# Where the second block's memory is projected, and in which order the first block's mixers get their projections

## Chip, cores and metric

One Trainium2 chip, one core of it. The metric is device time in microseconds (us), the median of repeated executions. The profile is one execution taken by the hardware profiler. PE is TensorE, DVE is VectorE, ACT is ScalarE, POOL is GpSimd, SP is the queue that issues most DMAs.

## What is computed

Two transformer blocks on 512 tokens of width 1024, all in float32 (batch 1, depth 1). The first block, cut to what matters:

```python
h = rms_norm(x, norm_mix_gain)
sb_q, sb_k, sb_v, hg_q, hg_f, hg_i, hg_g, mem_q = jnp.split(h @ w_in, split_points, axis=-1)
sb_o = rms_norm(stick_breaking_attention(sb_q, sb_k, sb_v), sb_out_gain)        # 8 heads of 64
hg_o = rms_norm(hgrn2_recurrence(hg_q, hg_f, hg_i, lb), hg_out_gain) * silu(hg_g)  # 4 heads, keys 128, values 64
mem_k, mem_v = jnp.split(rms_norm(mem, mem_norm_gain) @ w_mem_kv, 2, axis=-1)   # 256 memory rows
mem_o = memory_attention(mem_q, mem_k, mem_v, mem_q_gain, mem_k_gain)           # 4 heads
x = x + jnp.concatenate([sb_o, hg_o, mem_o], axis=-1) @ w_out
x = x + peer_ffn(rms_norm(x, norm_ffn_gain), ...)      # 16384 experts, 8 heads, 16 of them each
```

The second block, on the x that the first one leaves:

```python
q, k, v, qm, gate = split(rmsnorm(x, norm_g_2) @ w_in_2)
mix = dilated_window_mixer(q, k, v)                                # 3 groups of 4 heads
kv = rmsnorm(mem_2, mem_norm_g_2) @ w_mem_kv_2                     # does not depend on x
y = concat([mix, full_softmax_attention(qm, kv)]) * silu(gate)
out = rmsnorm(x + y @ w_out_2, final_norm_g_2)
```

## The kernel before

**Projections.** A float32 matrix product is made of three products of rounded halves (hi·hi, hi·lo, lo·hi). `weight` and `split` (L97 to L114) load one slice of a weight matrix, 1024 x 256, in two DMAs of 512 KB (`w_raw`, 3 buffers); ACT makes the upper half (L108), POOL or DVE the lower half (L109). In the first block there are two sets of `w_hi` and `w_lo`, so two slices are ready at a time; there POOL makes the lower halves. `mm_feat` (L116) gives a slice with features on the partitions: 2 groups of 24 matmuls with 512 columns. `mm_tok` (L126) gives it with tokens on the partitions: 4 groups of 24 matmuls with 256 columns. Both go over the input in 8 chunks of 128 features (kc). `to_feat` (L136) makes their input: per chunk it transposes the blocks of 128 rows on PE, then ACT writes the upper half (L151) and DVE the lower (L152).

**First block** (`first`, L421). The rows of x are loaded and normalized (`norm_rows`: square sum on ACT, a small operation on DVE, a power on POOL (L95), a product on DVE (L161)). All four blocks are transposed together, chunk by chunk. Then in the order of the program (L556 to L576): the recurrence's values `tok(10)`; `stick_in(0)`, which is query, key and value slice of the first half of the stick-breaking mixer (`feat(0)`, `feat(2)`, `tok(4)`); the mixer `stick(0)`; `hgrn_in(0)` (two slices for two heads of the recurrence); head 0; `stick_in(1)`; head 1; the rows of the memory; `stick(1)`; `hgrn_in(1)`; heads 2 and 3; the recurrence's gate `tok(11)`; the memory's queries `tok(12)` and `mem_q`; the memory's keys and values `mem_kv`; the second block's memory `mem_2`, whose result goes to DRAM (`kvd`); the memory attention `mem_out`; `hgrn_out`. `stick` works through 10 pairs of blocks (query block qb, key block kb): scores on PE (L285), a chain over DVE and ACT (L290 to L301), a cumulative sum on PE (L303 to L306), again DVE and ACT, and after each query block the product with the values (L314). A head of the recurrence has 7 levels, each of DVE, ACT and PE (L343 to L356). Then `to_feat(mixed)`, the output projection (four slices of `w_out`), and x is stored to DRAM (`x1`).

**What sets the order.** The program is written in one sequence; a scheduler, when the program is built, gives each engine its own fixed queue. An earlier line goes first where both are ready by its reckoning; work of later lines fills the rest. On the chip each queue runs in order. Tiles of one name share a fixed number of buffers (`bufs`), and a new tile waits until the old one has been read for the last time. For the change these matter: `sb_qz`, `sb_kT` and `sb_v` (2 buffers each: the mixer's inputs, and in turn the memory's rows), `hg_qf` (1 buffer: the recurrence's inputs, and before also the memory's upper half), the two weight sets.

**The loop of the experts** (`peer`, L653): 128 iterations over blocks of 128 experts, one product `first_product` (L625 to L627) until iteration 95 and 18 matmuls (L672) each. Beside it POOL gathers rows of `peer_u` and `peer_v` for the first token block (`gather`), and DVE multiplies and adds them (L882, L887). At iteration 100 `keep` (L685) takes the buffer `xT_hi` for x and loads three blocks of `x1` and the second block's projected memory.

**Second block** (`second`, L893): x is normalized (L912), transposed (L914), projected slice by slice from `tok(6)` on; `featT(0)` is next. Its lower halves are made on DVE.

Of the kernel before, what the change touches and what calls it, by code (L numbers as in the profile page):

```python
# [9 lines left out]
F32 = mybir.dt.float32  # L10
# [11 lines left out]
NB = S // P  # L22
# [63 lines left out]
class Body:  # L86
# [39 lines left out]
    def mm_tok(self, ps, w, xt, t0):  # L126

        nc = self.nc
        (wh, wl), (xh, xl) = w, xt
        for kc in range(KC):  # L130
            a, b = xh[:, kc, t0:t0 + P], xl[:, kc, t0:t0 + P]
            nc.tensor.matmul(ps, a, wh[:, kc, :], start=kc == 0, stop=False)  # L132
            nc.tensor.matmul(ps, a, wl[:, kc, :], start=False, stop=False)  # L133
            nc.tensor.matmul(ps, b, wh[:, kc, :], start=False, stop=kc == KC - 1)  # L134

    def to_feat(self, rows, nblk, hi, lo, gain, psums):  # L136

        nc = self.nc
        n = nblk * P
        for kc in range(KC):  # L140
            pool, tag = psums[kc % len(psums)]
            ps = pool.tile([P, 512], F32, name=tag)
            for b in range(nblk):
                nc.tensor.transpose(ps[:, b * P:(b + 1) * P], rows[b][:, kc * P:(kc + 1) * P], self.ident)
            src, h, l = ps[:, :n], hi[:, kc, :], lo[:, kc, :]
            if gain is None:
                nc.scalar.activation(h, src, AF.Copy)
                nc.vector.tensor_tensor(l, src, h.bitcast(F32), op=OP.subtract)
            else:
                g = self.vec[:, gain + kc:gain + kc + 1]  # L150
                nc.scalar.activation(h, src, AF.Copy, scale=g)  # L151
                nc.vector.scalar_tensor_tensor(l, src, g, h.bitcast(F32), op0=OP.mult, op1=OP.subtract)  # L152
# [54 lines left out]
    def mem_kv_2(self, xt, kT, v, wpool, psm):  # L207

        nc = self.nc
        wk = self.weight("w_mem_kv_2", 0, wpool, 2, nc.gpsimd)  # L210
        for c in range(2):
            ps = psm.tile([P, 512], F32, name="mm")
            self.mm_feat(ps[:, :256], wk, xt, c * P)
            nc.scalar.activation(kT[:, c, :], ps[:, :256], AF.Copy)
        wv = self.weight("w_mem_kv_2", 1, wpool, 2, nc.gpsimd)
        for b in range(2):
            ps = psm.tile([P, 512], F32, name="mm")
            self.mm_tok(ps[:, :256], wv, xt, b * P)
            nc.vector.tensor_copy(v[:, b, :], ps[:, :256])

# [53 lines left out]
    def stick(self, g, qz, kT, v, mixed, pool, psa, pso):  # L274
# [146 lines left out]
    def first(self, cp, gp, xr):  # L421
        nc, tc, A = self.nc, self.tc, self.A
        with ExitStack() as es:
# [40 lines left out]
            vi = pool.tile([P, NB, 256], F32, name="hg_i")  # L464
            rows = []
            for n in range(2):
                x2 = tp.tile([P, 2, D], F32, name="sb_qz", bufs=2)
                for b in range(2):
                    nc.sync.dma_start(x2[:, b], A["x"][(2 * n + b) * P:(2 * n + b + 1) * P, :])
                    r = xr.tile([P, D], F32, name="xrow", bufs=4)  # L470
                    self.norm_rows(x2[:, b], r, tp)
                    rows.append(r)
            self.to_feat(rows, NB, hi, lo, V_GMIX, [(psa, "att"), (phg, "hs")])
            mixed = [xr.tile([P, D], F32, name="xrow", bufs=4) for _ in range(NB)]

# [16 lines left out]
            def mem_2(xt):  # L492
                kT = tp.tile([P, 2, 256], F32, name="sb_kT", bufs=2)
                v = tp.tile([P, 2, 256], F32, name="sb_v", bufs=2)
                self.mem_kv_2(xt, kT, v, wpool, psm)
                nc.sync.dma_start(self.kvd[:, :2], kT)
                nc.sync.dma_start(self.kvd[:, 2:], v)
# [10 lines left out]
            def stick_in(eng, g):  # L508
                qz = tp.tile([P, 2, 2, S], F32, name="sb_qz", bufs=2)
                kT = tp.tile([P, 2, S], F32, name="sb_kT", bufs=2)  # L510
                v = tp.tile([P, NB, 256], F32, name="sb_v", bufs=2)
                self.zero_pads(qz, eng)
                feat(g, qz, 0.125)
                feat(2 + g, kT)
                tok(4 + g, slabs(v))
                return qz, kT, v
# [39 lines left out]
            tok(10, slabs(vi))  # L556
            sb = stick_in(nc.vector, 0)
# [3 lines left out]
            hin = hgrn_in(0)  # L561
            hgrn(0, *hin)
# [17 lines left out]
            self.to_feat(mixed, NB, hi, lo, V_GOUT, [(phg, "hs")])  # L580
# [3 lines left out]
            for i in range(4):  # L584
                w = self.weight("w_out", i, wpool)
                for b in range(NB):
                    ps = psm.tile([P, 512], F32, name="mm")
                    self.mm_tok(ps[:, :256], w, (hi, lo), b * P)
                    xs = self.x[b][:, i * 256:(i + 1) * 256]
                    nc.vector.tensor_tensor(xs, xs, ps[:, :256], op=OP.add)  # L590
# [4 lines left out]
    def peer(self, gp, er):  # L595

        nc, tc, A = self.nc, self.tc, self.A
        with ExitStack() as es:
# [46 lines left out]
            with ExitStack() as ec:  # L645
# [7 lines left out]
                for i in range(NE):  # L653
# [21 lines left out]
                    if i == NE - PRE + 4:  # L675
                        self.keep(gp)
# [8 lines left out]
    def keep(self, gp):  # L685
# [4 lines left out]
        for b in range(1, NB):  # L690
# [3 lines left out]
        nc.sync.dma_start(kv, self.kvd)  # L694
# [198 lines left out]
    def second(self):  # L893
        nc, tc, A = self.nc, self.tc, self.A
        with ExitStack() as es:
# [18 lines left out]
            self.to_feat(rows, NB, hi, lo, V_GN2, [(psa, "att")])  # L914
# [199 lines left out]
    def build(self):  # L1114
        nc, tc, A = self.nc, self.tc, self.A
        with ExitStack() as es:
            cp = es.enter_context(tc.tile_pool(name="const", bufs=1, reuse_waits="tile"))
            nc.scalar.preload_act_table_set("natural_log_exp_and_others")
# [13 lines left out]
            self.kvd = dp.tile([P, 4, 256], F32, name="kvd")  # L1132
# [5 lines left out]
            self.second()  # L1138

# [63 lines left out]
```

## Time and profile before

| | us |
|---|---|
| median of 3 runs | 2050.05 (2048.04 to 2053.41) |
| the profiled execution, own time | 2051.2 |
| its span, first to last instruction | 2049.1 |

The profiled execution lies 2.1 us above its span and 1.15 us above the median. In this profile a matmul's end is modelled and neighbours overlap, so what a run of matmuls takes is read from starts, or from a stretch that holds nothing else. "Busy" is the union of an engine's instructions in a stretch. PEclk is the granted TensorE clock as a share of the upper of its two levels (2.4 GHz; the lower is 1.2 GHz). A row of the timeline has the start, the duration, engine, line, operation, output and inputs with shapes, the count, and in brackets the idle time of the engine before it and what ended it.

### The profile page before, as it was taken

How to read it: one execution, taken by the hardware profiler on the slowest of the kernel's cores; microseconds unless marked ns; L12 is line 12 of the kernel's file. 1: busy time of each engine (PE TensorE's matmuls, PEld its weight loads, DVE VectorE, ACT ScalarE, POOL GpSimd, SP SyncE). 2: the span in 40 equal slices, each digit the busy share in tenths (PEclk: the TensorE clock that was granted, in tenths of full speed). 3: DMA queues.
4: the chain of work that ended last, by engine and by line, in shares of the span. 5: the costliest groups of instructions: out<-in, count | busy, mean ns of one | idle time of the engine just before them, and what ended most of it. 6: DMA issues, size and time to landing. Idle time of an engine off the chain costs nothing.

```text
span 2049.1 us, 29902 instructions
## 1 busy us (share of the span) xinstructions
PE 1922.6 (94%) x11285; PEld 1751.1 (85%) x11285; DVE 1413.5 (69%) x2670; ACT 871.8 (43%) x1365; POOL 674.5 (33%) x523
## 2 busy tenths in 40 slices
PE   7999988989688999999999999999999999899997
PEld 6778777989688899899999999999999787789897
DVE  3486875369998976686777777777877676433463
ACT  4564645254346666333333333333433333343442
POOL 4324233076452230043434344334433342113100
PEclk9999999999888999999999999999999999999998
DMA  4211113354324445998889988999898886223211
GB/s 163 71 63 42 42 42 122 122 169 135 103 93 156 184 178 193 311 350 301 295 310 313 316 289 307 316 314 315 308 324 277 279 285 228 93 73 103 74 63 52
DMA packets 150239, 398.19 MB, mean 194 GB/s; under 512 B 12368, under 2 KB 61520, under 8 KB 146896
## 3 DMA queue, kind: packets, MB, share of 16 engines
q1 hardware_dynamic: 110608, 257.83, 37.7%
q0 software_dynamic: 38912, 136.37, 18.5%
q8 instruction: 88, 1.44, 0.3%
q10 hardware_dynamic: 576, 2.10, 0.3%
q14 instruction: 55, 0.45, 0.1%
HBM read 364.23 MB, written 29.88 MB: 192 GB/s over the span
## 4 chain that ended last, share of the span: by engine, by line
PE 61%; DVE 11%; DMA 4%; issue 2%; ACT 1%; POOL 1%; DVEq 0%; POOLq 0%; ACTq 0%
PE o L672 22%; PE hp L626 7%; PE hp L627 7%; PE hp L625 7%; DMA g_row<-peer_v,idx 3%; PE mm L132 2%; PE mm L122 2%; PE mm L123 2%; PE mm L124 2%; PE mm L133 2%; PE mm L134 2%; DVE gated L847 1%; PE g L853 1%; PE g L854 1%; PE mm L854 1%
## 5 line engine op out<-in xcount | busy, mean ns | idle before, releaser
L108 ACT ACTIVATE w_hi<-w_raw 128x1024 fp32r<-128x1024 f32 x366 | 385.7, 1059 | 604.1 <-DMA w_raw<-peer_v 194.4
L109 DVE TENSOR_TENSOR w_lo<-w_raw,w_hi 128x1024 fp32r<-128x1024 f32 x268 | 326.1, 1220 | 92.2 <-ACT w_hi L108 91.5
L625 PE MATMUL hp<-xT_hi,w_hi 128*128 128x384 f32 x1024 | 350.4, 342 | 20.0 <-ACT act L629 20.0
L626 PE MATMUL hp<-xT_lo,w_hi 128*128 128x384 f32 x1024 | 349.5, 341 | 0.0
L627 PE MATMUL hp<-xT_hi,w_lo 128*128 128x384 f32 x1024 | 348.4, 340 | 0.0
L109 POOL TENSOR_TENSOR w_lo<-w_raw,w_hi 128x1024 fp32r<-128x1024 f32 x98 | 245.3, 2511 | 251.5 <-ACT w_hi L108 248.2
L878 POOL DMA_INDIRECT g_row<-peer_u,idx x128 | 169.5, 1324 | 354.5 <-PE o L672 121.5
L878 POOL DMA_INDIRECT g_row<-peer_v,idx x128 | 168.5, 1316 | 264.7 <-PE o L672 116.1
L672 PE MATMUL o<-w_hi,wl 128*128 128x512 f32 x768 | 239.9, 394 | 6.2 <-DVE wl L667 6.2
L672 PE MATMUL o<-w_hi,wh 128*128 128x512 f32 x768 | 240.3, 394 | 2.6 <-ACT wh L666 2.6
L672 PE MATMUL o<-w_lo,wh 128*128 128x512 f32 x768 | 238.8, 392 | 0.0
L882 DVE SCALAR_TENSOR_TENSOR g_row<-g_row,kv 128x1024 f32<-128x1024 f32 x128 | 156.2, 1223 | 94.4 <-DMA g_row<-peer_u,idx 93.8
L625 PEld LDWEIGHTS hp<-xT_hi,w_hi 128*128 128x128 f32 x1024 | 195.9, 191 | 24.2 <-ACT act L629 20.6
L626 PEld LDWEIGHTS hp<-xT_lo,w_hi 128*128 128x128 f32 x1024 | 195.9, 191 | 3.6
L627 PEld LDWEIGHTS hp<-xT_hi,w_lo 128*128 128x128 f32 x1024 | 195.7, 191 | 0.0
L887 DVE SCALAR_TENSOR_TENSOR x<-g_row,dots,x 128x1024 f32<-128x1024 f32 x103 | 132.2, 1283 | 71.6 <-DMA g_row<-peer_v,idx 71.3
L672 PEld LDWEIGHTS o<-w_hi,wl 128*128 128x128 f32 x768 | 144.9, 189 | 38.9 <-DVE wl L667 7.8
L672 PEld LDWEIGHTS o<-w_lo,wh 128*128 128x128 f32 x768 | 145.2, 189 | 32.3
L672 PEld LDWEIGHTS o<-w_hi,wh 128*128 128x128 f32 x768 | 144.0, 189 | 27.2 <-ACT wh L666 2.9
L666 ACT ACTIVATE wh<-act 128x384 fp32r<-128x384 f32 x128 | 67.0, 524 | 221.1 <-PE o L672 220.0
L122 PE MATMUL mm<-xT_hi,w_hi 128*128 128x256 f32 (+1 forms) x384 | 128.8, 336 | 0.4 <-ACT xT_hi L151 0.4
L123 PE MATMUL mm<-xT_lo,w_hi 128*128 128x256 f32 (+1 forms) x384 | 126.2, 329 | 0.0
(340 smaller groups left out, 3881.9 us busy)
## 6 DMA issues: line engine op xcount, KB each, us to landing
w_raw<-peer_uT SPq DMA_DIRECT2D x128, 512.0 KB
w_raw<-peer_v SPq DMA_DIRECT2D x128, 512.0 KB
w_raw<-w_in SPq DMA_DIRECT2D x54, 512.0 KB
gd<-stage SPq DMA_DIRECT2D x24, 1024.0 KB
gt<-gd SPq DMA_DIRECT2D x16, 1536.0 KB
w_raw<-w_query SPq DMA_DIRECT2D x32, 512.0 KB
w_raw<-w_out SPq DMA_DIRECT2D x16, 512.0 KB
w_raw<-w_mem_kv SPq DMA_DIRECT2D x8, 512.0 KB
```

Of the source, the lines that this page charges most:

```text
L108: nc.scalar.activation(hi[:, sl], raw, AF.Copy)
L109: eng.tensor_tensor(lo[:, sl], raw, hi[:, sl].bitcast(F32), op=OP.subtract)
L122: nc.tensor.matmul(ps, a, xh[:, kc, :], start=kc == 0, stop=False)
L123: nc.tensor.matmul(ps, a, xl[:, kc, :], start=False, stop=False)
L625: nc.tensor.matmul(ps, uh[:, kc, :], hi[:, kc, P:], start=kc == 0, stop=False)
L626: nc.tensor.matmul(ps, uh[:, kc, :], lo[:, kc, P:], start=False, stop=False)
L627: nc.tensor.matmul(ps, ul[:, kc, :], hi[:, kc, P:], start=False, stop=kc == KC - 1)
L666: nc.scalar.activation(wh, w, AF.Copy)
L672: last = nc.tensor.matmul(out[b][n], s_[:, sl], m_[:, n * 512:(n + 1) * 512], start=i == 0 and m_ is vh and s_ is wh, stop=i == NE - 1 and ...
L878: dma = nc.gpsimd.indirect_dma_start(out=u, out_offset=None, in_=A["peer_v" if k >= P else "peer_u"], in_offset=bass.IndirectOffsetOnAxis( ...
L882: nc.vector.scalar_tensor_tensor(u, u, 1.0, self.h2, op0=OP.mult, op1=OP.mult, accum_out=dots[:, c:c + 1])
L887: nc.vector.scalar_tensor_tensor(y, u, dots[:, c:c + 1], x, op0=OP.mult, op1=OP.add)
```

## The change

The second block's memory is no longer projected in the first block. In the loop (`keep`) its rows are loaded, normalized and transposed; at the head of `second` its weights are loaded before x is normalized and the products are made after that, before x is transposed. `kvd` is gone. In the first block, `stick_in` makes only queries and keys; the values are projected inside `stick`, after the scores of the first query block. `tok(10)` follows `hgrn_in(0)`. x is transposed in two pairs of blocks. The first memory (`mem_kv`, `tok(12)`, `mem_q`) comes between heads 2 and 3; its upper half lies in buffers of `sb_kT` and `sb_v` (`Halves`) instead of `hg_qf`. `tok(11)` follows `mem_out`. The output projection takes the chunks in the order 0, 1, 2, 3, 6, 7, 4, 5.

```diff
-    def to_feat(self, rows, nblk, hi, lo, gain, psums):
+    def to_feat(self, rows, nblk, hi, lo, gain, psums, group=None, order=range(KC)):
...
+        for b0 in range(0, nblk, group or nblk):
+            here = range(b0, b0 + (group or nblk))
+            t = slice(b0 * P, (b0 + len(here)) * P)
+            for kc in order:
...
+                h, l = hi[:, kc, t], lo[:, kc, t]
...
     def mem_kv_2(self, xt, kT, v, wpool, psm):
-        wk = self.weight("w_mem_kv_2", 0, wpool, 2, nc.gpsimd)
+        wk, wv = (self.weight("w_mem_kv_2", i, wpool, 2, nc.gpsimd) for i in range(2))
+        yield
         for c in range(2):
...
-        wv = self.weight("w_mem_kv_2", 1, wpool, 2, nc.gpsimd)
         for b in range(2):
...
+        yield
...
-    def stick(self, g, qz, kT, v, mixed, pool, psa, pso):
+    def stick(self, g, qz, kT, values, mixed, pool, psa, pso):
...
                 at[kb] = z
+            if qb == 0:
+                v = values()
             for h in range(4):
...
             def mem_in(rows, gain):
-                hi = pool.tile([P, KC, 256], F32R, name="hg_qf", bufs=1)
+                hi = Halves(*(tp.tile([P, KC // 2, 256], F32R, name=n, bufs=2) for n in ("sb_kT", "sb_v")))
                 lo = tp.tile([P, KC, 256], F32R, name="sb_qz", bufs=2)
...
-            self.to_feat(rows, NB, hi, lo, V_GMIX, [(psa, "att"), (phg, "hs")])
+            self.to_feat(rows, NB, hi, lo, V_GMIX, [(psa, "att"), (phg, "hs")], 2)
...
-            tok(10, slabs(vi))
-            sb = stick_in(nc.vector, 0)
+            sb = stick_in(nc.gpsimd, 0)
...
             hin = hgrn_in(0)
+            tok(10, slabs(vi))
             hgrn(0, *hin)
...
             hgrn(2, *hin)
-            hgrn(3, *hin)
-            tok(11, slabs(hg))
+            self.mem_kv(mem_in(normal, V_GMEM), kTm, vm, tp, wpool, psm, pst)
             tok(12, mq)
             mqz = mem_q()
-            self.mem_kv(mem_in(normal, V_GMEM), kTm, vm, tp, wpool, psm, pst)
-            mem_2(mem_in(mem_rows("mem_2"), V_GMEM2))
+            hgrn(3, *hin)
             mem_out(mqz)
+            tok(11, slabs(hg))
             hgrn_out()
...
-            self.to_feat(mixed, NB, hi, lo, V_GOUT, [(phg, "hs")])
+            order = [0, 1, 2, 3, 6, 7, 4, 5]
+            self.to_feat(mixed, NB, hi, lo, V_GOUT, [(phg, "hs")], order=order)
...
-    def keep(self, gp):
+    def keep(self, gp, psh):
...
-        for b in range(1, NB):
+        m = gp.tile([P, 2, KC, 256], F32R, name="xT_lo")
+        rows = []
+        for b, (src, dst) in enumerate(((1, 3), (2, 1))):
+            nc.sync.dma_start(self.x[src], A["mem_2"][b * P:(b + 1) * P, :])
+            self.norm_rows(self.x[src], self.x[dst], self.small)
+            rows.append(self.x[dst])
+        self.mem2 = m[:, 0], m[:, 1]
+        self.to_feat(rows, 2, *self.mem2, V_GMEM2, [(psh, "hp")])
+        for b in (2, 1, 3):
             nc.sync.dma_start(self.x[b], self.x1[b])
         kv = gp.tile([P, 4, 256], F32, name="kv")
-        nc.sync.dma_start(kv, self.kvd)
...
     def second(self):
...
-            b1 = pool.tile([P, 2, 512], F32, name="b1")
-            nc.sync.dma_start(b1, A["c_b1"].rearrange("p (g c) -> p g c", g=2))
-            gfin = pool.tile([P, D], F32, name="gfin")
-            nc.sync.dma_start(gfin, A["g_final"].to_broadcast([P, D]))
             kTm, vm = self.kv2
+            memory = self.mem_kv_2(self.mem2, kTm, vm, wpool, psm)
+            next(memory)
...
                 self.norm_rows(self.x[b], r, px)
                 rows.append(r)
+
+            next(memory)
+            b1 = pool.tile([P, 2, 512], F32, name="b1")
+            nc.sync.dma_start(b1, A["c_b1"].rearrange("p (g c) -> p g c", g=2))
+            gfin = pool.tile([P, D], F32, name="gfin")
+            nc.sync.dma_start(gfin, A["g_final"].to_broadcast([P, D]))
             self.to_feat(rows, NB, hi, lo, V_GN2, [(psa, "att")])
```

## Rows read from the trace of the kernel before

**Rows 1.** The page: the span.

```profile
span 2049.1 us, 29902 instructions
```

**Rows 2.** Stretches: length, busy time of each engine, PEclk, DMA share, GB/s.

```profile
0.00:22.40 22.40, 9.04 (x43) 7.44 (x44) 12.38 (x26) 13.09 (x20) 10.73 (x17) 1.00 0.69 243
22.40:66.70 44.30, 44.30 (x281) 39.89 (x280) 5.03 (x11) 11.53 (x15) 18.50 (x8) 1.00 0.29 99
66.70:170.10 103.40, 96.70 (x538) 79.78 (x537) 70.33 (x133) 63.03 (x103) 36.70 (x32) 1.00 0.20 62
170.10:293.00 122.90, 108.45 (x681) 96.03 (x680) 101.36 (x205) 67.16 (x109) 36.54 (x52) 0.94 0.11 35
293.00:368.60 75.60, 63.13 (x445) 57.11 (x444) 46.49 (x99) 41.58 (x91) 23.26 (x16) 0.93 0.33 112
368.60:413.50 44.90, 44.79 (x371) 44.31 (x369) 13.46 (x25) 8.16 (x11) 3.47 (x3) 1.00 0.35 130
1577.00:1754.80 177.80, 171.62 (x761) 142.91 (x759) 119.31 (x126) 59.88 (x80) 58.69 (x44) 0.98 0.74 253
1754.80:1770.00 15.20, 8.41 (x40) 6.81 (x41) 11.30 (x19) 9.06 (x16) 4.89 (x4) 0.66 0.47 171
```

**Rows 3.** Stretches that hold one kind of work: two slices by mm_feat, one by mm_tok, mem_2.

```profile
32.70:55.20 22.50, 22.50 (x99) 18.09 (x98) 0.42 (x1) 7.11 (x10) 9.53 (x4) 1.00 0.28 94
55.20:66.70 11.50, 11.50 (x98) 11.50 (x97) 1.28 (x3) 2.49 (x3) 4.76 (x2) 1.00 0.27 91
334.00:349.00 15.00, 14.67 (x116) 14.11 (x115) 9.88 (x25) 6.38 (x15) 3.03 (x3) 0.96 0.16 54
293.00:322.30 29.30, 21.53 (x158) 20.03 (x157) 14.26 (x32) 15.66 (x28) 14.14 (x9) 0.94 0.18 58
```

**Rows 4.** Timeline of PE: first and last of the first mixer's ten cumulative sums.

```profile
74.09 0.50 PE L303 MATMUL att<-sb_h,tri 128*128 128x512 f32 x1 [1.69 <-ACT sb_h L300]
...
141.26 0.50 PE L303 MATMUL att<-sb_h,tri 128*128 128x512 f32 x1
```

**Rows 5.** Waits of PE from 170.1 to 293 us, the longest.

```profile
PE hs L339 <- DVE hg_kt L355: 10.7, 4, 3.9
```

**Rows 6.** Timelines of SP and ACT: the memories' weights, issued and converted.

```profile
207.06 111.61 SPq L106 DMA_DIRECT2D w_raw<-w_mem_kv  x8
...
296.96 1.06 ACT L108 ACTIVATE w_hi<-w_raw 128x1024 fp32r<-128x1024 f32 x1 [2.05 <-POOL hr_r L95]
```

**Rows 7.** Groups of lines, DVE from 66.7 to 368.6 us, ACT from 293 to 349 us.

```profile
L152 DVE SCALAR_TENSOR_TENSOR sb_qz<-hs,vec,hg_qf 128x256 fp32r<-128x256 f32 x16 | 7.4, 479 | 5.6 <-ACT hg_qf L151 5.6
L161 DVE TENSOR_SCALAR sb_kT<-sb_qz,rs 128x1024 f32<-128x1024 f32 x2 | 1.5, 753 | 1.3 <-POOL rs L95 1.3
L151 ACT ACTIVATE hg_qf<-hs,vec 128x256 fp32r<-128x256 f32 x16 | 7.2, 471 | 2.7 <-PE hs L144 2.6
```

**Rows 8.** Timelines of PE, ACT and POOL around the loop's end.

```profile
1758.54 1.12 PE L144 MATMUL att<-cst,xrow 128*128 128x128 f32 x4 [3.77 <-DVE rs_t L94]
1766.06 0.58 PE L132 MATMUL mm<-w_hi,yT_hi 128*128 128x256 f32 x1
1780.60 0.40 PE L122 MATMUL mm<-yT_hi,w_hi 128*128 128x512 f32 x1
...
1747.34 2.96 ACT L108 ACTIVATE w_hi<-w_raw 128x1024 fp32r<-128x1024 f32 x3 [0.63 <-DVE wl L667]
...
1756.29 1.41 POOL L95 TENSOR_TENSOR rs<-rs_t,mhalf 128x1 f32<-128x1 f32 x1 [7.62 <-DVE rs_t L94]
```

**Rows 9.** Timelines of POOL and DVE while the rows of x are normalized.

```profile
13.63 2.34 POOL L109 TENSOR_TENSOR w_lo<-w_raw,w_hi 128x1024 fp32r<-128x1024 f32 x1
16.63 0.95 POOL L230 MEMSET sb_qz<- 64x1024 f32 x1 [0.66 <-POOL w_lo L109]
...
14.03 2.49 DVE L161 TENSOR_SCALAR xrow<-sb_qz,rs 128x1024 f32<-128x1024 f32 x1
17.81 0.75 DVE L152 SCALAR_TENSOR_TENSOR xT_lo<-att,vec,xT_hi 128x512 fp32r<-128x512 f32 x1 [1.29 <-ACT xT_hi L151]
```

More of the change, by code (lines that the diff above doesn't have):

```diff
@@ L124, in mm_feat, with mm_tok @@
             nc.tensor.matmul(ps, b, xh[:, kc, :], start=False, stop=kc == KC - 1)
-    def mm_tok(self, ps, w, xt, t0):
+    def mm_tok(self, ps, w, xt, t0, order=range(KC)):
         nc = self.nc
         (wh, wl), (xh, xl) = w, xt
-        for kc in range(KC):
+        for n, kc in enumerate(order):
             a, b = xh[:, kc, t0:t0 + P], xl[:, kc, t0:t0 + P]
-            nc.tensor.matmul(ps, a, wh[:, kc, :], start=kc == 0, stop=False)
+            nc.tensor.matmul(ps, a, wh[:, kc, :], start=n == 0, stop=False)
@@ L133, in mm_tok @@
             nc.tensor.matmul(ps, a, wl[:, kc, :], start=False, stop=False)
-            nc.tensor.matmul(ps, b, wh[:, kc, :], start=False, stop=kc == KC - 1)
-    def to_feat(self, rows, nblk, hi, lo, gain, psums):
+            nc.tensor.matmul(ps, b, wh[:, kc, :], start=False, stop=n == KC - 1)
+    def to_feat(self, rows, nblk, hi, lo, gain, psums, group=None, order=range(KC)):
         nc = self.nc
[L139 to L152, printed above, removed]
+        turn = count()
+        for b0 in range(0, nblk, group or nblk):
+            here = range(b0, b0 + (group or nblk))
+            t = slice(b0 * P, (b0 + len(here)) * P)
+            for kc in order:
+                pool, tag = psums[next(turn) % len(psums)]
+                ps = pool.tile([P, 512], F32, name=tag)[:, :len(here) * P]
+                for i, b in enumerate(here):
+                    nc.tensor.transpose(ps[:, i * P:(i + 1) * P], rows[b][:, kc * P:(kc + 1) * P], self.ident)
+                h, l = hi[:, kc, t], lo[:, kc, t]
+                if gain is None:
+                    nc.scalar.activation(h, ps, AF.Copy)
+                    nc.vector.tensor_tensor(l, ps, h.bitcast(F32), op=OP.subtract)
+                else:
+                    g = self.vec[:, gain + kc:gain + kc + 1]
+                    nc.scalar.activation(h, ps, AF.Copy, scale=g)
+                    nc.vector.scalar_tensor_tensor(l, ps, g, h.bitcast(F32), op0=OP.mult, op1=OP.subtract)
@@ L462, in hgrn_in @@
                 return both[:, 0], both[:, 1]
[L464 to L472, printed above, removed]
-            self.to_feat(rows, NB, hi, lo, V_GMIX, [(psa, "att"), (phg, "hs")])
-            mixed = [xr.tile([P, D], F32, name="xrow", bufs=4) for _ in range(NB)]
             def mem_rows(name):
@@ L490, in mem_in @@
                 return hi, lo
[L492 to L497, printed above, removed]
+            vi = pool.tile([P, NB, 256], F32, name="hg_i")
+            rows = []
+            for n in range(2):
+                x2 = tp.tile([P, 2, D], F32, name="sb_qz", bufs=2)
+                for b in range(2):
+                    nc.sync.dma_start(x2[:, b], A["x"][(2 * n + b) * P:(2 * n + b + 1) * P, :])
+                    r = xr.tile([P, D], F32, name="xrow", bufs=4)
+                    self.norm_rows(x2[:, b], r, tp)
+                    rows.append(r)
+            self.to_feat(rows, NB, hi, lo, V_GMIX, [(psa, "att"), (phg, "hs")], 2)
+            mixed = [xr.tile([P, D], F32, name="xrow", bufs=4) for _ in range(NB)]
             def hgrn(j, hq, hf):
@@ L514, in stick_in, with values @@
                 feat(2 + g, kT)
-                tok(4 + g, slabs(v))
-                return qz, kT, v
+                def values():
+                    v = tp.tile([P, NB, 256], F32, name="sb_v", bufs=2)
+                    tok(4 + g, slabs(v))
+                    return v
+                return qz, kT, values
             def stick(g, sb):
@@ L587, in first @@
                     ps = psm.tile([P, 512], F32, name="mm")
-                    self.mm_tok(ps[:, :256], w, (hi, lo), b * P)
+                    self.mm_tok(ps[:, :256], w, (hi, lo), b * P, order)
                     xs = self.x[b][:, i * 256:(i + 1) * 256]
@@ L675, in peer @@
                     if i == NE - PRE + 4:
-                        self.keep(gp)
+                        self.keep(gp, psh)
                     if SKIP <= i < NE - LAST:
@@ L689, in keep @@
         self.x = [x[:, b] for b in range(NB)]
-        for b in range(1, NB):
+        m = gp.tile([P, 2, KC, 256], F32R, name="xT_lo")
+        rows = []
+        for b, (src, dst) in enumerate(((1, 3), (2, 1))):
[5 more added lines that the diff above has]
+        for b in (2, 1, 3):
             nc.sync.dma_start(self.x[b], self.x1[b])
@@ L1117, in build @@
             cp = es.enter_context(tc.tile_pool(name="const", bufs=1, reuse_waits="tile"))
+            self.small = cp
             nc.scalar.preload_act_table_set("natural_log_exp_and_others")
@@ L1138, in build, with __init__, __getitem__ @@
             self.second()
+class Halves:
+    def __init__(self, *two):
+        self.two = two
+    def __getitem__(self, at):
+        p, kc, cols = at
+        return self.two[kc // 4][p, kc % 4, cols]
 def own(ps):
```

2 lines of the change are left out of this document (removed).

## The prediction

> **What bounds the kernel now.** I read the stretches first, then stretches that hold one kind of work, then waits and timelines. PE carries nearly the whole span [rows 1, 2]: the loop's tail has it busy 171.62 of 177.80 us, the output projection 44.79 of 44.90. The change touches 0 to 368.6 us (the first block up to its output projection) and a strip around the loop's end; the rest keeps its work and its length. From 22.4 to 368.6 us, 346.2 us, PE is busy 44.30 + 96.70 + 108.45 + 63.13 = 312.6 us and idle 33.6 [rows 2]. The first mixer (66.7 to 170.1) is 93.5% busy, because later projections fill PE while DVE and ACT work; from 170.1 to 368.6 it is 86.4%, and the granted clock is 0.94 and 0.93: part of that time ran at 1.2 instead of 2.4 GHz. What PE lost to that I estimate from the missing share, 0.06 x 122.9 + 0.07 x 75.6 = 12.7 us. The recurrence makes PE wait for DVE 10.7 us [rows 5], and after 293 us hardly any projections are left to fill with.
>
> **The price list.** Two slices by mm_feat take 22.5 us of PE, one by mm_tok 11.5 [rows 3]. The second memory's 96 matmuls and most of its 16 transposes stand in 334 to 349 us with 14.67 us busy [rows 3]; taking the matmuls off as one mm_tok slice (as many matmuls, as wide) leaves 3.2 us for 20 small matmuls, 0.16 each.
>
> **First block.** *Taken out:* 14.7 us of PE, in a place where PE is the engine the memory attention waits for. With it go about 6 us of DVE, 11 of ACT and 10 of POOL (halves and normalizations at the prices of [rows 6, 7, 9]), all beside it, two loads of rows, the loads of its weights and two stores on SP; SP waits for buffers there rather than for bandwidth (DMA share 0.16), so I count these at nothing.
>
> *Reordering.* It moves PE work, it doesn't remove any. The work left in 22.4 to 368.6 us is 312.6 - 12.7 - 14.7 = 285.2 us, so at most 346.2 - 285.2 = 61.0 us can go. Two projections instead of four stand ahead of the first mixer: its chain starts near 44 us instead of 66.7. Its ten block pairs follow each other by (141.26 - 74.09) / 9 = 7.5 us [rows 4], a chain of DVE and ACT with room for fill on PE. The values tok(4) now stand in PE's queue ahead of the second query block's scores (11.5 us, of which one pair covers 7.5), but they no longer hold back the whole mixer; the same with tok(5) for the second mixer. tok(10) becomes fill, needed only at the end of head 0. The first memory and tok(12) become fill for head 3, where rows 5 stem from. So the sparse second half should become like the dense first mixer: at its 93.5% and the upper clock, 285.2 us of work take 305.0, 41.2 us less than 346.2. The ends are 14.7 (all idle time moves elsewhere) and 61.0 (none is left); I take the density of the first mixer, as it is the one row of mixers run with enough fill, and deduct 3 us for the next point: 38.
>
> *A new wait.* mem_kv takes both weight sets, but its input lies in the second buffers of sb_kT, sb_v and sb_qz, free only when the second mixer is done. Before, tok(11) and tok(12) ran meanwhile, and the memories' weights, issued from 207.06 us on, were converted from 296.96 on [rows 6]. Now tok(12) and tok(11) queue behind mem_kv's sets, so PE has no projection to fill with between feat(7) and the end of the second mixer. Bounds: nothing (mixer and head 2 get PE sooner) and 23 us (two mm_tok slices pushed out); 3 us, near the low end, since DVE is busy 101.36 of 122.9 us there and sets the pace anyway.
>
> *Start.* Once the last rows are there, DVE writes 8 lower halves of 256 columns at 0.479 us [rows 7] instead of 512 at 0.75 [rows 9]: 2.2 us less. ACT has 16 instead of 8 upper halves, most of them early. The clears of the mixer's input go from DVE to POOL, 2 x 0.95 us ahead of feat(0)'s lower halves [rows 9]. Between 0 and 2.2 gained; I take 1. The chunk order of the output projection lets six chunks start before the recurrence's two; hidden either way unless the gate is last, so nothing.
>
> **Loop.** Added at iteration 100: two loads of 512 KB (one of 512 KB goes), two normalizations, 16 transposes, 8 pairs of halves. PE: 16 x 0.16 = 2.5 us in a stretch where PE sets the pace; I take 2. DVE gets some 2 x 0.9 + 8 x 0.479 = 5.6 us beside 119.31 busy of 177.8, ACT 8 x 0.47 [rows 7] and two square sums beside 59.88: covered. Two powers on POOL (up to 1.41 us [rows 8]) stand among the row gathers. On SP the loads of x1 wait for the transposes with peer_v's loads behind them; the 5 sets of peer_v halves cover 5 iterations of 18 x 171.62 / 761 = 4.1 us, 20 us. If PE meets the transposes before the rows are normalized it stands still: ends 0 and 10 us (two and a half iterations, half the cover).
>
> **After the loop.** PE waits 3.77 us for the first normalized rows; from 1754.8 to 1770 it is busy 8.41 of 15.2 us at a granted clock of 0.66, and tok(6), begun at 1766.06, ends at 1780.60 [rows 2, 8]. Now the 96 matmuls fill this: 1754.8 + 11.5 = 1766.3, then 32 transposes at 0.16 to 1771.4, then tok(6) to 1782.9: 2.3 us later than before. Their weights: the first upper halves can be made at 1747.34 [rows 8]; POOL needs 4 x 2.34 us for the lower ones [rows 9], to some 1758, so the second slice (from 1760.6) has them. The first power stood at 1756.29 on POOL and now has lower halves ahead of it; DVE, freed of tok(6)'s lower halves, can make up for some. tok(6) gets its set when the first slice is through, 1760.6, and 4.6 us of ACT and DVE later it is ready: covered by the second slice and the transposes. One product of the normalization (L161) took 2.49 us beside POOL's lower half, 0.753 alone [rows 7, 9]; one such hit is 1.7. In all 4 us lost; the ends are 0 and 15 (11.5 uncovered, plus two hits).
>
> The Trainium skill (SBUF — State Buffer, "Who interferes with whom") says that such an operation and GpSimd exclude each other for the whole instruction. By that rule all four products could be hit, 7 us instead of 1.7; this trace's pair agrees with the rule.
>
> A second rule of the skill speaks against the gap the new wait makes (TensorE: Matmul & The Clock Gate, "Why this matters for your kernels"): pauses of PE bring the clock down. The 0.66 after the loop agrees [rows 2]. By it the gap costs more than its length, while the one after the loop becomes cheaper.
>
> **Sum.** 38 + 1 - 2 - 4 = 33 us off the profiled execution's own 2051.2 us: 2018. That execution lies 1.15 us above the median, so 2017.
>
> **Rivals.**
> *A, the slack goes wholly:* 61.0 + 1 - 2 - 4 = 56 us, 1994. For it: chains start 20 us earlier than now. Against it: DVE is already 82% busy in 170.1 to 293.
> *B, DVE sets the pace of the recurrence anyway:* idle time only moves; 14.7 + 1 - 2 - 4 = 10 us, 2040. For it: rows 5. Against it: in the first mixer DVE is busy only 68%.
> *C, the projection after the loop isn't covered,* so that it does not do what it is moved for: 15 instead of 4, 2028. For it: POOL has both the lower halves and the powers. Against it: PE's idle time there is real.
> *D, slower: the weight sets.* If mem_kv holds both sets until head 3 is nearly done, tok(12) and tok(11) come after it: 293 + 29.3 (the memory's stretch [rows 3]) + 23 + 31.6 (the last stretch less 29.3 and less 14.7) = 376.9 instead of 368.6; with loop and strip 13 us slower, 2063. It decides from a first memory product at about 284 us. Against it: the second mixer starts some 20 us earlier than now, and its end should move with its start.
>
> **Numbers.** Forecast 0.50, A 0.16, B 0.13, C 0.13, D 0.08. The range leaves out D and the edges of A and B: 1993 to 2042. About 0.3% (6 us) can be told from no change; half of B falls within it: faster 0.50 + 0.16 + 0.13 + 0.07 = 0.86, same 0.06, slower 0.08.
>
> **What would show it.** The output projection begins near 330 us instead of 368.6, with PE over 90% busy and the clock near 1 from 170 us on; the first mixer's first cumulative sum near 51 us; the first memory's products at 240 to 260 us. In the loop's tail the 16 transposes with little idle ahead of them. Behind the loop no PE gap above 2 us, and featT(0)'s first matmul within 5 us of 25.8 us after the loop's last. Wrong would be: PE idle for 10 us and more while both weight sets are held, an output projection later than 355 us, or a PE wait on the normalized memory in the loop.

## The result and the profile after

The changed kernel takes 2068.4 us (median of 4 runs, 2060.9 to 2072.4), the kernel before 2049.7 in runs beside it: ratio 1.0093, interval 1.0073 to 1.0113. It is 19 us slower where 33 us less was forecast. The profiled execution is the fastest of the four; its span is 10 us longer than before, so it understates the loss.

The page's first line and the stretches of the changed kernel (length, busy time of PE, PEld, DVE, ACT, POOL, PEclk, DMA share, GB/s); the last two are the loop's tail and the strip behind it:

```profile
span 2059.1 us, 29916 instructions
```

```profile
22.40:66.70 44.30, 41.01 (x228) 35.00 (x226) 13.47 (x21) 17.01 (x25) 20.62 (x10) 1.00 0.28 96
66.70:170.10 103.40, 94.10 (x530) 78.10 (x530) 71.06 (x129) 59.58 (x94) 32.62 (x31) 1.00 0.19 58
170.10:293.00 122.90, 103.29 (x631) 88.98 (x632) 86.95 (x181) 65.97 (x109) 36.23 (x45) 0.96 0.13 42
293.00:366.80 73.80, 62.05 (x458) 56.39 (x457) 44.28 (x106) 32.40 (x74) 15.10 (x18) 0.98 0.14 42
366.80:415.00 48.20, 43.91 (x357) 43.46 (x355) 14.26 (x26) 8.28 (x12) 3.46 (x3) 0.96 0.42 156
1584.60:1762.40 177.80, 170.93 (x769) 141.86 (x768) 122.47 (x137) 64.13 (x90) 60.16 (x46) 0.99 0.72 251
1762.40:1777.60 15.20, 14.11 (x117) 13.51 (x115) 11.92 (x17) 11.08 (x18) 7.45 (x7) 1.00 0.72 247
```

Beside [rows 2]: 14.7 us of PE work are gone, yet the output projection ends at 415.1 instead of 413.5. No stretch of the first block became clearly denser: 41.01 of 44.30 us where all 44.30 were busy, 94.10 instead of 96.70 in the next, 84% instead of 88% busy from 170.1 to 293, and 84% as before from there to the output projection. Only the strip behind the loop is as forecast, 14.11 of 15.20 us busy instead of 8.41.

The timeline of PE shows four signs: the first mixer's first cumulative sum, the first product of the first memory, head 3's first and second level and its next one, and the output projection going on behind a pause:

```profile
51.89 0.50 PE L307 MATMUL att<-sb_h,tri 128*128 128x512 f32 x1 [0.81 <-ACT sb_h L304]
...
269.55 0.37 PE L132 MATMUL mm<-w_hi,sb_kT 128*128 128x256 f32 x1
...
280.07 1.06 PE L345 MATMUL hs<-hg_qf 128*128 128x128 f32 x8
280.96 1.06 PE L345 MATMUL hs<-hg_qt,hg_kt 128*128 128x128 f32 x8
...
306.19 1.95 PE L345 MATMUL hs<-hg_qt,hg_kt 128*128 128x128 f32 x16
...
373.69 0.58 PE L132 MATMUL mm<-w_hi,xT_hi 128*128 128x256 f32 x1 [4.25 <-DVE xrow L593]
374.07 0.41 PE L133 MATMUL mm<-w_lo,xT_hi 128*128 128x256 f32 x1
374.28 0.41 PE L134 MATMUL mm<-w_hi,xT_lo 128*128 128x256 f32 x1
```

The first mixer starts as early as forecast (51 us). Then the lead is gone: the memory's products come at 269.55, and between 282.0 and 306.2 head 3 has no level, since the memory, `tok(12)` and the queries stand ahead of it in PE's queue. At the end PE waits 4.25 us inside the output projection: 48 of its 384 matmuls are done, and the next ones need a buffer that DVE frees when it adds x (L593).

Two suspects offer themselves: that hole of 24 us, and the late projections. A third, `tok(11)` behind the memory attention, moved in the same edit, and the text before the run had it only within the upper end of the new wait.

### The profile page after: what moved, and what is told of

It is laid out like the page before. It is cut to its first block, busy times and chain, and to the rows that moved or that the text cites. A ratio compares the mean times of both kernels' runs of the same rounds, so it can differ in the third digit from the quotient of the medians.

```text
span 2059.1 us, 29916 instructions
## 1 busy us (share of the span) xinstructions
PE 1923.2 (93%) x11285; PEld 1751.4 (85%) x11285; DVE 1416.5 (69%) x2676; ACT 876.3 (43%) x1373; POOL 662.9 (32%) x525
## 4 chain that ended last, share of the span: by engine, by line
PE 61%; DVE 13%; issue 5%; DMA 4%; POOL 2%; ACT 2%; POOLq 0%; DVEq 0%; SPq 0%; ACTq 0%
PE o L675 20%; PE hp L628 7%; PE hp L630 7%; PE hp L629 7%; PE mm L132 3%; DMA g_row<-peer_v,idx 3%; PE mm L134 3%; PE mm L133 3%; PE mm L123 2%; PE mm L122 2%; PE mm L124 2%; DVE gated L858 1%; PE g L864 1%; POOL w_lo L109 1%; PE g L865 1%
## 5 line engine op out<-in xcount | busy, mean ns | idle before, releaser
L889 POOL DMA_INDIRECT g_row<-peer_v,idx x128 | 159.1, 1243 | 271.1 <-PE o L675 154.1
L123 PE MATMUL mm<-xT_lo,w_hi 128*128 128x256 f32 (+1 forms) x400 | 130.7, 327 | 0.0
```

Of the source, the lines that this page charges most:

```text
L123: nc.tensor.matmul(ps, a, xl[:, kc, :], start=False, stop=False)
L889: dma = nc.gpsimd.indirect_dma_start(out=u, out_offset=None, in_=A["peer_v" if k >= P else "peer_u"], in_offset=bass.IndirectOffsetOnAxis( ...
```

## The experiments

All ratios are to the kernel before, from runs on the same chip. A difference between two experiments is the difference of their ratios times 2049 us. "First block ends" is the end of the output projection's last matmul in the one profile of each kernel.

| | us | ratio (95%) | first block ends |
|---|---|---|---|
| before, first profile | 2049.7 | 1 | 413.5 |
| changed, first profile | 2068.4 | 1.0093 (1.0073 to 1.0113) | 415.1 |
| E1 changed again | 2070.6 | 1.0111 (1.0085 to 1.0136) | 421.0 |
| E2 memory behind both heads | 2057.2 | 1.0044 (1.0021 to 1.0066) | 409.6 |
| E3 values first | 2061.8 | 1.0084 (1.0057 to 1.0111) | 409.8 |
| **E4 first block as before, less the second memory** | 2040.6 | 0.9963 (0.9946 to 0.9980) | 394.6 |
| E5 E4 + memory amid | 2059.4 | 1.0045 (1.0031 to 1.0059) | 411.9 |
| E6 E4 + late projections | 2052.6 | 1.0021 (1.0003 to 1.0039) | 405.9 |
| E7 E4 + x by pairs | 2040.4 | 0.9956 (0.9932 to 0.9979) | 391.0 |
| E8 E4 + transposes spread | 2039.1 | 0.9940 (0.9921 to 0.9959) | 392.6 |
| E9 E5, head 3 ahead of the memory | 2070.6 | 1.0106 (1.0088 to 1.0125) | 422.8 |
| **E10 E5, `tok(11)` ahead of the attention** | 2039.3 | 0.9953 (0.9935 to 0.9970) | 391.1 |
| E11 E4 + `tok(10)` late | 2042.7 | 0.9977 (0.9957 to 0.9998) | 392.3 |
| E12 E8, fill behind head 3 | 2045.8 | 0.9994 (0.9979 to 1.0008) | 401.6 |
| **E13 changed, `tok(11)` ahead** | 2054.1 | 1.0035 (1.0018 to 1.0052) | 410.1 |
| E14 E4 + `tok(5)` late | 2052.3 | 1.0000 (0.9983 to 1.0016) | 399.3 |
| E15 E4 + `tok(4)` late | 2046.5 | 0.9983 (0.9972 to 0.9994) | 393.6 |
| E16 the parts that cost nothing | 2037.1 | 0.9940 (0.9919 to 0.9960) | 393.2 |

**E1. The changed kernel again.** No edit.

> The changed kernel as it is, once more, to see how far its own time spreads. Three theories stand beside each other for the missing 33 us. T1 (memory amid): with the first memory's projection, tok(12) and the memory's queries ahead of head 3, head 3's cumulative sums stand behind them in PE's queue (a hole of 24 us between two of its levels), and tok(11) and the recurrence's output come in series at the end. T2 (late values): four projections no longer ahead of the mixers make both mixers' own projections later work, so feats 9, 7 and heads 1 and 2 come some 16 us later than before. T3 (loop and strip): the first block is even and the time is lost behind it. All three: 2061 to 2072 us, output projection at 415 us as in the changed kernel's first profile.

2070.6 us; the first block of this profile ends at 421.0, 6 us later than in the first one. Single profiles place a difference; the ratios size it.

**E2. The memory behind both heads.**

```diff
             hgrn(2, *hin)
-            self.mem_kv(mem_in(normal, V_GMEM), ...)
+            hgrn(3, *hin)
+            tok(11, slabs(hg))
             tok(12, mq)
             mqz = mem_q()
-            hgrn(3, *hin)
+            self.mem_kv(mem_in(normal, V_GMEM), ...)
             mem_out(mqz)
-            tok(11, slabs(hg))
```

> Changed kernel with the first memory behind both heads again (head 2, head 3, tok(11), tok(12), queries, memory, its attention, the recurrence's output). T1: 2045 to 2050 us, output projection starts 15 to 20 us earlier than the changed kernel's 366.8. T2: 2063 or more, the start of the output projection moves by less than 5 us. T3: 2066 to 2070, nothing moves.

1.0044: 14 us (against E1) come back, short of T1's number. The edit undoes two things, the memory's place and that of `tok(11)`; E9 and E10 part them.

**E3. Values ahead of the mixers, `tok(10)` first.**

```diff
+            tok(10, slabs(vi))
             sb = stick_in(nc.gpsimd, 0)
...
-            tok(10, slabs(vi))
...
-                def values():
-                    v = ...
-                    tok(4 + g, slabs(v))
-                    return v
-                return qz, kT, values
+                v = ...
+                tok(4 + g, slabs(v))
+                return qz, kT, lambda: v
```

> Changed kernel with tok(10) first and the values projected ahead of the mixers as before; the memory stays ahead of head 3. T1: 2065 us or more, the hole in head 3 stays. T2: about 2052, feats 9 and 7 are through near 222 us instead of 237 and the output projection starts some 15 us earlier. T3: 2066 to 2070.

1.0084: between T1 and T2, 5.5 us better than E1, hardly more than the intervals. Neither half alone is the cause.

**E4. The first block in its old order.** Order, buffers, clears, chunk order and transposes of the first block are those of before, without `mem_2`; `keep` and `second` are those of the changed kernel.

> The first block wholly in the order of the kernel before, without the second memory in it; the second memory in the loop and behind it as in the changed kernel. T1 and T2: the kernel before less the second memory's 14.7 us of PE plus 2 in the loop and 2 to 4 behind it, about 2040 (2035 to 2045), output projection at about 354 us. T3: 2055 or more.

2040.6 us, as T1 and T2 said. So moving the second memory past the loop pays 7.6 us (interval 4.1 to 11.1), and the rest of the change costs 27 to 30 (1.0093 or 1.0111 less 0.9963). T3 falls as the cause of that. In E4's profile the first block ends 18.9 us earlier than before, more than the 14.7 taken out; by the ratio some 11 us of it are lost again behind the first block.

**E5 to E7. One part of the rest each, put into E4.** E5:

```diff
-                hi = pool.tile([P, KC, 256], F32R, name="hg_qf", bufs=1)
+                hi = Halves(...)
...
             hgrn(2, *hin)
-            hgrn(3, *hin)
-            tok(11, slabs(hg))
+            self.mem_kv(mem_in(normal, V_GMEM), ...)
             tok(12, mq)
             mqz = mem_q()
-            self.mem_kv(mem_in(normal, V_GMEM), ...)
+            hgrn(3, *hin)
             mem_out(mqz)
+            tok(11, slabs(hg))
```

E6, with `values` as in the changed kernel, and E7:

```diff
-                return qz, kT, lambda: v
+                return qz, kT, values
...
-            tok(10, slabs(vi))
...
             hin = hgrn_in(0)
+            tok(10, slabs(vi))
```

```diff
-            self.to_feat(rows, NB, hi, lo, V_GMIX, [(psa, "att"), (phg, "hs")])
+            self.to_feat(rows, NB, hi, lo, V_GMIX, [(psa, "att"), (phg, "hs")], 2)
```

> The faster kernel of the last runs (first block in the order of before, 2040.6 us) with one part of the change put in: the first memory, tok(12) and the queries between heads 2 and 3, tok(11) after the memory attention, upper half in the buffers of sb_kT and sb_v. Theory M (this order costs by itself): 2050 to 2056 us, head 3 begins near 274 us instead of 257 and the output projection ends near 407 instead of 394.5. Theory O (what the two half-undone kernels still had in common, that is the transposes by pairs, the clears on POOL and the chunk order, is what costs): 2039 to 2043.

> The faster kernel with another single part put in: the values projected inside the mixers and tok(10) after hgrn_in(0). Theory V (late values cost by themselves, because head 2 waits for its projections): 2050 to 2056 us, head 2 begins near 240 us instead of 221, the output projection ends near 408. Theory O: 2039 to 2043.

> The faster kernel with the rows of x transposed by pairs of blocks, and nothing else. M and V: 2038 to 2043, since the first scores move by no more than 2 us either way. O: 2048 or more, or at least 5 us above 2040.6.

E5 costs 17 us (0.0082 x 2049), E6 12, E7 nothing (first scores at 65.92 us instead of 66.17). The two costs together, 29 us, are all that the change lost beside E4, so O falls as their cause. Of O's three parts only the pairs were tried alone. Kernels that hold all three lie above kernels that do the rest without them: E3 8 us above E5, E2 4.7 above E6, E13 2.9 above E6 (its order of the memory costs nothing, see E10), while the changed kernel lies within 2 us of E4 and the two costs. Whether the clears on POOL or the chunk order cost a few us stays open. (The profiles don't settle it: E3's is of an execution of 2058.1 us, E5's of one of 2067.5, the other way round than their medians.) What in E5's edit costs was still a guess: M names the delay of head 3.

**E8. The transposes in the loop, one chunk per iteration.**

```diff
                     if i == NE - PRE + 4:
-                        self.keep(gp, psh)
+                        kept = self.keep(gp, psh)
+                    if NE - PRE + 4 <= i <= NE - PRE + 4 + KC:
+                        next(kept)
...
-        self.to_feat(rows, 2, *self.mem2, V_GMEM2, [(psh, "hp")])
+        for kc in range(KC):
+            yield
+            self.to_feat(rows, 2, *self.mem2, V_GMEM2, [(psh, "hp")], order=[kc])
...
+        yield
```

> The faster kernel with the 16 transposes in the loop spread: one chunk at each of eight iterations instead of all eight in one, and the loads of x after them. Theory W (the loop's loss of 2 to 8 us is the two buffers of hp that wait for lower halves standing in DVE's queue behind gathered rows): the wait of 3.1 us ahead of the third pair of transposes goes, 2036 to 2039. Rival (the loss is the transposes' own PE time and the supply of peer_v): 2040 to 2042.

Waits of PE around the loop's tail, of the changed kernel and then of E8; between them DVE's timeline in the changed kernel at that wait:

```profile
PE hp L147 <- DVE xT_lo L155: 3.0, 1, 3.0
PE o L675 <- DVE wl L670: 2.3, 4, 1.6
PE o L675 <- ACT wh L669: 1.5, 1, 1.5
```

```profile
1646.08 1.28 DVE L898 SCALAR_TENSOR_TENSOR xT_hi<-g_row,dots,x 128x1024 f32<-128x1024 f32 x1 [1.06 <-DMA g_row<-peer_v,idx]
1647.28 0.55 DVE L670 TENSOR_TENSOR wl<-act,wh 128x384 fp32r<-128x384 f32 x1
1647.75 1.22 DVE L109 TENSOR_TENSOR w_lo<-w_raw,w_hi 128x1024 fp32r<-128x1024 f32 x1
1648.89 0.87 DVE L155 SCALAR_TENSOR_TENSOR xT_lo<-hp,vec,xT_lo 128x256 fp32r<-128x256 f32 x2
```

```profile
PE o L672 <- ACT wh L666: 4.0, 1, 4.0
PE o L672 <- DVE wl L667: 3.2, 2, 2.7
PE att L147 <- DVE yT_lo L155: 1.0, 1, 1.0
```

The third pair of transposes needs a buffer of `hp`; the lower half that frees it stands in DVE's queue behind a gathered row that is still arriving. With the chunks spread, that wait is gone from E8 (others have come, 4.0 and 3.2 us on `wh` and `wl`). From its first to its last product the loop takes 922.0 to 926.8 us in the three profiles with spread chunks and 923.3 to 935.3 (mean 929.0) in the fourteen without. The ratio, 0.0023 better than E4, is within both intervals: W's mechanism is shown, its gain is not resolved.

**E9, E10. Which half of E5's edit.**

The first diff is E9, the second E10, both against E5:

```diff
             hgrn(2, *hin)
+            hgrn(3, *hin)
             self.mem_kv(mem_in(normal, V_GMEM), ...)
             tok(12, mq)
             mqz = mem_q()
-            hgrn(3, *hin)
             mem_out(mqz)
             tok(11, slabs(hg))
```

```diff
             hgrn(3, *hin)
+            tok(11, slabs(hg))
             mem_out(mqz)
-            tok(11, slabs(hg))
```

> The kernel with the first block's order of before (2040.6 us), with the memory, tok(12) and the queries moved up as in the change and its upper half in the other buffers, but head 3 placed ahead of them; tok(11) stays after the memory attention. Theory H (the cost of the memory amid is that it stands ahead of head 3 in PE's queue): 2038 to 2045, head 3 begins near 257 us. Theory L (the cost is tok(11) and the recurrence's output in series after the memory attention): 2050 to 2058.

> The memory, tok(12) and the queries ahead of head 3 as in the change, but tok(11) straight behind head 3, ahead of the memory attention. H: 2053 to 2060, head 3 still stands still for about 20 us behind the memory and tok(12). L: 2040 to 2047.

H falls, twice. E10 keeps the hole (no level of head 3 from 274.7 to 296.3) and costs nothing beside E4; E9 closes it and is 12.5 us slower than E5. L holds: the place of `tok(11)` is the whole cost (E9 lies above L's 2058, for a second reason, below). The hole in E10, head 3's first levels and the next:

```profile
273.46 1.05 PE L345 MATMUL hs<-hg_qf 128*128 128x128 f32 x8
274.35 0.39 PE L345 MATMUL hs<-hg_qt,hg_kt 128*128 128x128 f32 x2
...
296.34 0.83 PE L345 MATMUL hs<-hg_qt,hg_kt 128*128 128x128 f32 x6
```

PE's projections that read the upper half `xT_hi` (two of each three matmuls) in E10, then in E5 (length, busy time and matmuls recorded, PEclk, DMA share, GB/s):

```profile
294.00:320.00 26.00, 13.47 (x66) 1.00 0.13 42
320.00:341.00 21.00, 0.00 (x0) 1.00 0.09 29
341.00:353.30 12.30, 8.45 (x45) 1.00 0.82 289
353.30:369.00 15.70, 15.70 (x90) 1.00 0.19 72
```

```profile
294.00:320.00 26.00, 0.20 (x2) 0.93 0.12 38
320.00:341.00 21.00, 0.86 (x5) 1.00 0.02 5
341.00:353.30 12.30, 11.52 (x64) 1.00 0.00 0
353.30:369.00 15.70, 5.45 (x29) 0.94 0.74 247
```

In E10 `tok(11)` runs beside head 3; the memory attention follows, and the output projection is dense from 346.4 us on. In E5 head 3 has nothing beside it, `tok(11)` stands alone in 341 to 353.3 with no transfer under way (DMA share 0.00), and then come, one after the other, the recurrence's gate, its transposes and the loads of x, which take the buffers that those transposes read. SP, DVE and PE of E5 show that end:

```profile
361.52 3.12 SPq L583 DMA_DIRECT2D xrow<-x  x4
...
368.79 0.42 DVE L590 TENSOR_TENSOR xrow<-xrow,mm 128x256 f32<-128x256 f32 x1 [5.46 <-DMA xrow<-x]
...
369.26 0.58 PE L132 MATMUL mm<-w_hi,xT_hi 128*128 128x256 f32 x1 [5.22 <-DVE xrow L590]
```

So the 20.8 us by which E5's output projection ends later (411.9 against 391.1) are 12.3 of `tok(11)` alone, 5.2 of this pause, and some 2 of a slower clock behind it (20 matmuls at 0.21 us from one to the next instead of 0.12); about 1 is left over.

E9's extra loss is the weight sets. All projections by mm_feat or mm_tok that PE makes, in E9 and then in E10:

```profile
222.00:257.00 35.00, 0.00 (x0) 0.85 0.10 31
257.00:285.00 28.00, 0.00 (x0) 0.83 0.00 1
```

```profile
222.00:257.00 35.00, 0.00 (x0) 0.80 0.10 31
257.00:285.00 28.00, 17.15 (x115) 1.00 0.12 38
```

ACT and PE of E9: the second set is filled with the memory's weights, the memory's first product, and the next conversion of weights:

```profile
218.31 2.01 ACT L108 ACTIVATE w_hi<-w_raw 128x1024 fp32r<-128x1024 f32 x2
...
287.01 0.37 PE L132 MATMUL mm<-w_hi,sb_kT 128*128 128x256 f32 x1
...
296.77 1.99 ACT L108 ACTIVATE w_hi<-w_raw 128x1024 fp32r<-128x1024 f32 x2
```

Both kernels stand without a projection from 222 to 257 us: both sets belong to the memory, whose input is not there. In E9 head 3 comes next, so it is 63 us, at a clock of 0.85 and 0.83.

**E11, E14, E15. One late projection each, put into E4.** E11 moves `tok(10)` alone behind `hgrn_in(0)`; the others project the values late for one mixer alone, E14 for the second (below), E15 for the first (0 in place of 1):

```diff
+                if g == 1:
+                    return qz, kT, values
+                v = values()
                 return qz, kT, lambda: v
```

> The order of before with tok(10) alone moved behind hgrn_in(0); the values stay ahead of the mixers. Late projections cost 12 us together. If a projection put behind the mixer's start is simply done later, at a lower density of PE, in proportion to how many are moved: 2044 to 2048, the first scores at about 55 us, head 2 at about 228. If only the values inside the mixers matter: 2039 to 2042. If only tok(10) does: 2050 or more.

> The order of before (2040.6 us) with tok(5) alone projected inside the second mixer. In the kernel with all late values head 1 ran with tok(5) as fill and feat(9) and feat(7) came some 20 us later, so head 2 began at 243 instead of 221. If tok(5) is the one that costs: 2047 to 2053, head 2 near 235. If it is tok(4) in the first mixer: 2039 to 2043.

> The order of before with tok(4) alone projected inside the first mixer. If tok(4) is the one that costs: 2047 to 2053, the first mixer begins near 55 us but ends no earlier than 149 less 4. If it is tok(5): 2039 to 2044, like tok(10) moved alone (2042.7).

2.9, 7.6 and 4.1 us beside E4; their sum, 14.6, is about E6's 11.9. The 2.9 are within the intervals, and the 4.1 hardly more. The second mixer's `tok(5)` is the largest, and the only one that its profile shows in the first block (399.3 us); what `tok(10)` and `tok(4)` cost by their ratios is not found there. First the stretch of E4 that holds `tok(5)` (busy time of PE, PEld, DVE, ACT, POOL), then PE around head 1's third level in E4 and in E14:

```profile
148.00:169.40 21.40, 21.40 (x143) 19.64 (x143) 10.06 (x30) 7.63 (x13) 9.29 (x7) 1.00 0.26 79
```

```profile
169.40 1.05 PE L345 MATMUL hs<-hg_qf 128*128 128x128 f32 x8
170.29 2.17 PE L345 MATMUL hs<-hg_qt,hg_kt 128*128 128x128 f32 x16
...
176.45 2.68 PE L345 MATMUL hs<-hg_qt,hg_kt 128*128 128x128 f32 x16 [2.65 <-DVE hg_kt L361]
```

```profile
163.91 0.28 PE L132 MATMUL mm<-w_hi,xT_hi 128*128 128x256 f32 x1
169.52 3.67 PE L345 MATMUL hs<-hg_qt,hg_kt 128*128 128x128 f32 x16 [5.33 <-DVE hg_kt L361]
172.93 0.39 PE L133 MATMUL mm<-w_lo,xT_hi 128*128 128x256 f32 x1
```

In E4 `tok(5)` runs dense, without a chain to wait for. In E14 four of its matmuls are issued, then PE stands 5.33 us for the head's level, with the other 92 ready behind it: the queue doesn't go round the level. feat(9) and feat(7), the two slices of `hgrn_in(1)`, follow later, and head 2 begins at 235.3 instead of 220.7.

**E12. Fill behind head 3 and ahead of the attention.** Order: heads 2 and 3, memory, `tok(12)`, queries, `tok(11)`, attention; with E8's edit and `Halves`.

> Head 3, then memory, tok(12), queries, tok(11), memory attention; with the transposes in the loop spread over eight iterations. H, and fill for head 3 and for the memory attention taken from behind them: 2033 to 2039, the best so far. Rival (the fill was as good before): 2039 as with the spread transposes alone.

Neither forecast holds: E12 is 11 us behind E8 (0.0054 x 2049), for E9's reason: head 3 runs unfilled behind held weight sets, and PE makes no projection from 222 to 285 us.

**E13. One line of the changed kernel.**

```diff
+            tok(11, slabs(hg))
             mem_out(mqz)
-            tok(11, slabs(hg))
```

> The changed kernel with one line moved: tok(11) ahead of the memory attention. If the two costs (tok(11) behind the attention, 19 us; values and tok(10) late, 12 us) are separate and add up: 2048 to 2053 us, output projection ends near 401. If the late values eat the same fill and leave nothing for tok(11) to fill: 2060 or more. If tok(11) was the whole cost in this order: 2042 or less.

12 us come back against the first runs of the changed kernel, 15.6 against E1, a little under E5's 17. The rest over E4, 14.8 us, is E6's 12 and no more than the intervals beside it. So the costs add up, though the first block of this profile ends at 410.1, not near 401.

**E16. The parts that cost nothing.** E10 with E7's pairs and E8's spread chunks.

> The parts that did not cost, together: values first, x by pairs, memory ahead of head 3 with tok(11) straight behind head 3, transposes in the loop spread. 2035 to 2039 if the small gains of each (1.3 and 1.5 us) add up; 2039 to 2042 if they are noise.

2037.1 us, 0.9940: 12 us under the kernel before and the lowest median of the study; the ratio is E8's. Its gain over E4 and E10 is not resolved.

## Why the prediction was wrong

**The second memory: right in the sum, by luck in its terms.** The terms of the text for this part alone, 14.7 less 2 and less 4, give 8.7 us; E4 gained 7.6. But its first block ends 18.9 us earlier, not 14.7, and more is lost behind it than the 6 of the text. In the fourteen profiles with the chunks at once, what follows the first block takes 5.4 to 21.6 us longer than in the one profile of before, 12.8 in the mean: 2.5 between first block and loop, where the change touches nothing, 7.5 in the loop, 2.8 behind it. What causes the 2.5, and most of the 7.5, is not shown.

**The step that failed is "Reordering",** 23 of the 38 us, which came out as a loss of 27 to 30. Its sum held that late projections become fill and the sparse half takes the density of the first mixer. Three sentences of it:

- "The first memory and tok(12) become fill for head 3." They became a block ahead of it (no level from 282.0 to 306.2 us). That cost nothing (E10), but it brought nothing.
- `tok(11)` behind the attention had no sentence of its own. The new wait's bounds had "two mm_tok slices pushed out", 23 us, and 3 were taken. Head 3 had lost its fillers, and the end of the block became a chain without cover: 17 us (E5 against E4), 19 (E5 against E10).
- The values "no longer hold back the whole mixer". True, and worth nothing: the first sum came 22 us earlier, at 51.89 instead of 74.09 [rows 4], but the mixer ended only 8.7 us earlier (140.7 instead of 149.4). What the end of the block waits for is head 2 and head 3, and behind them the last projections. Ahead of the mixers PE made projections at its full rate; inside them it makes them between waits. 12 us (E6).

The text noted that moving removes no PE work, and still took 26.5 us of idle time and lower clock as gained (41.2 less the 14.7 that are taken out). Rival B, "idle time only moves", 2040 us at 0.13, has the number that the best orders reach: 2040.6, 2039.3, 2037.1.

**The new wait,** as the text saw it, is there: in the changed kernel PE makes no projection from 237.6 to 269.5 us, in E9 and E10 none for 35 us and more, while the memory holds both sets. Where the memory is next in the queue it costs nothing that the times show (E10), and 11 to 12.5 us where head 3 is (E9, E12). One reading behind it was wrong: before, the first of the memory's weights were converted at 270.52 us (the 27th conversion, behind 26 loads of `w_in`); 296.96 [rows 6] is that of its third load.

**Rival D** gave 2063 us, near the result, by another way: the first memory product came at 269.55, not 284, and E10 holds the sets as long at 2039.3.

**Start,** 1 us: nothing from the pairs (E7); the clears on POOL were not tried alone. **Loop,** 2 us with ends of 0 and 10: 0.5 to 14 us longer than the 921.5 of the one profile of before, mean 7.5 with the chunks at once, 2.8 with them spread. The wait was the hinted one in kind, but for a buffer behind a gathered row, not for normalized rows. **Strip,** 4 us: featT(0) begins 28.15 us behind the loop's last product in the changed kernel, 2.3 later than 25.8; that is the bare sum of PE's matmuls. In three of the seventeen profiles it is 4.5 to 4.7. Of the normalization's four products in the changed kernel one took 2.89 us beside a lower half on POOL, one 1.42 beside a clear on POOL, and two 0.75; the long ones end some 0.55 us behind POOL's instruction. The rule of the Trainium skill (SBUF — State Buffer, "Who interferes with whom"), by which all could be held up for a whole instruction, fits these two. PE had other work meanwhile (14.11 of 15.20 us).

## What to carry to other kernels

Work that fills an in-order queue is worth what stands beside it in the queue, not its place in the program: for each projection that is moved ask which chain loses its filler, and what runs alone at the new place. Give every moved line a price, the last one in the block above all, since behind it there is nothing left to cover. Here a chain that started 20 us earlier gained nothing, since the end hung on another chain, and the dense stretch ahead of it was not idle time.

## What the runs showed of the hardware

Behind two pauses PE ran at the lower of its two levels, a granted clock of 0.50. PE's matmuls there, in the changed kernel and then in E14 (length, busy time, PEclk, DMA share, GB/s):

```profile
373.69:376.42 2.73, 2.73 (x13) 0.50 0.89 362
169.52:172.90 3.38, 3.38 (x16) 0.50 0.43 145
```

Behind 4.25 us the output projection's matmuls come every 0.21 us instead of 0.12, for 13 matmuls, some 1.2 us in all; behind 5.33 us the 16 matmuls of a level take 3.67 us instead of 1.95. The pauses themselves cost more than the clock. Not expected was how far the loop's length spreads between kernels whose loop is the same: 923.3 to 935.3 us, most of it behind iteration 95 (145.0 to 154.1 us there, 776.8 to 781.8 ahead of it). Two profiles of the changed kernel itself differ by 4.8 us (925.5 and 930.3). Why is not settled.
